# Six split halves of weights instead of four, with raw weights loaded in 1024-column halves

## The chip, the cores and the metric

The kernel runs on one core of one Trainium2 chip. The metric is the device time of one execution in microseconds (us), the median of several runs.

## What is computed

The reference takes 256 tokens of width 1024 through four layers, all in float32. The first block has two layers: a hybrid mixer (sliding-window attention beside a chunked gated delta rule) and a recurrent mixer (a gated linear recurrence), each followed by a layer norm and an MLP with a squared ReLU. The second block has two layers with latent attention, a 31-tap and a 3-tap convolution branch and another such MLP, modulated by vectors that come from large modulation weights; its first layer also carries 256 context tokens.

```python
def sqrelu_mlp(x, w1, w2):
    h = jax.nn.relu(x @ w1)
    return (h * h) @ w2
```

Nearly all the work is x @ w of this kind. The weights are read once each: about 190 MB of layer weights and 50 MB of modulation weights.

## The kernel before

**Products in three passes.** Each float32 operand is split into a rounded high part and the low remainder. A product is then three matmuls: high by high, high by low, low by high. The weights arrive in float32 and are split on the chip.

**Units and halves.** The host packs the weights into units of up to 2048 columns by 128 partitions (1 MB), in the order of their use. Each unit is split in two halves of up to 1024 columns. w_load starts the DMA of a whole unit into one of two raw tiles (tag wr, line 387). w_split takes the next half: ScalarE copies it to the high tile wh (line 407), VectorE subtracts to get the low tile wl (line 408). wh and wl have NW = 4 buffers each. w_next hands out one unit; it first loads one unit further (`while WS.nd < min(u + 2, nus)`) and splits one half further than its own unit (`while WS.nsp < min(first[u + 1] + 1, len(halves))`).

**What frees a buffer.** A raw tile comes free when both of its halves have been split, so the next load waits on VectorE's line 408. A wh or wl buffer comes free when TensorE has done the last matmul that reads it.

**Order of the work.** The program is written as one long list with generators that are woven together by hand. A planner then lays the instructions on the five engine queues: it follows the written order as priority, by its own model of when operands and buffers are ready. high_priority(ahead) moves the splits up that order by ahead places (60 in the mixers of the first block, 0 or as given elsewhere). On the chip each queue runs strictly in the order it was given. All DMAs are issued from one queue, SP: weights, modulation weights (tag wm, line 737, 512 KB each), rows of gains (line 448) and constants.

**Stages.** From about 225 to 425 us, 525 to 690 us and 1460 to 1625 us run the MLPs of 256 tokens, where each weight half is used once; from 950 to 1290 us an MLP over 512 tokens, where each half is used longer. Between them lie the mixers. At each passage into an MLP or mixer the function head (line 534) needs two whole units, that is four halves, at once, and its input comes through a chain on VectorE and ScalarE: layer norm (lines 660 to 670) or post_norm and normed (lines 1389 to 1426), transposes on TensorE (line 366), then to_xT (lines 645 to 649). tm1024 (line 501) is the last product before such a passage; its last two units are read until its very end.

Of the kernel before, what the change touches and what calls it, by code (L numbers as in the profile page):

```python
# [10 lines left out]
F32 = mybir.dt.float32  # L11
# [4 lines left out]
P = 128  # L16
BIG = 1.0e30
SM = 1.0 / math.sqrt(96.0)
NW = 4
LEAD = 96  # L20
TRAIL = 24
ALPHA = 4.0 ** 0.25
# [271 lines left out]
def hybrid_then_mla(ctx: ExitStack, tc: tile.TileContext, a, out, usizes):  # L294
    nc = tc.nc
    V, S, G, T = nc.vector, nc.scalar, nc.gpsimd, nc.tensor
    cpool = ctx.enter_context(tc.tile_pool(name="cpool", bufs=1))
    wpool = ctx.enter_context(tc.tile_pool(name="wpool", bufs=1))
# [39 lines left out]
    def f(ap):  # L338
        return ap.bitcast(F32)
# [32 lines left out]
    nus = len(usizes)  # L372
    halves = []
# [3 lines left out]
    first = [min(n for n, h in enumerate(halves) if h[0] == u) for u in range(nus)] + [len(halves)]  # L377

    def w_load():
        i = WS.nd  # L380
        WS.nd += 1
        r = wpool.tile([P, 2048], F32, tag="wr", bufs=2, name=f"wr{i}")
        n = usizes[i][0]
        parts = 2 if i < 2 else 1
        for j in range(parts):
            o = n // parts * j
            nc.sync.dma_start(out=r[:, o : o + n // parts], in_=a["wp"][i, :, o : o + n // parts])
            if i == 0:
                x_load(j)
        WS.raw[i] = r  # L390

    def x_load(q):
        nc.sync.dma_start(out=xT0[:, 2 * q : 2 * q + 2], in_=a["xT"][:, 2 * q : 2 * q + 2])

    def w_split():
        i = WS.nsp
        WS.nsp += 1
        u, o, n = halves[i]
        while WS.nd <= u:
            w_load()  # L400
        r = WS.raw[u][:, o : o + n]
        h = wpool.tile([P, 1024], F32R, tag="wh", bufs=NW, name=f"wh{i}")
        l = wpool.tile([P, 1024], F32R, tag="wl", bufs=NW, name=f"wl{i}")
        if u in WS.vec:
            V.tensor_copy(h[:, :n], r)
        else:
            S.copy(h[:, :n], r)  # L407
        V.tensor_tensor(l[:, :n], r, f(h[:, :n]), op=SUB)  # L408
        WS.hl[i] = (h[:, :n], l[:, :n])

    class Weights:

# [11 lines left out]
    def w_next(nk, ahead=None):  # L424

        ahead = WS.ahead if ahead is None else ahead
        u = WS.ng
        WS.ng += 1
        assert usizes[u][1] == nk
        while WS.nd < min(u + 2, nus):  # L430
            w_load()
        with tc.high_priority(ahead):
            while WS.nsp < min(first[u + 1] + 1, len(halves)):
                w_split()
        return Weights(nk, [WS.hl.pop(i) for i in range(first[u], first[u + 1])])

    w_load()
    x_load(2)
    x_load(3)
# [37 lines left out]
    def fm_unit(xTs, emit):  # L477

        w = w_next(8)
        for si, xT in enumerate(xTs):  # L480
            ps = psA()
            for m in range(2):
                for k in range(8):
                    fm_acc(ps[:, 256 * m : 256 * m + 256], xT, k, w, k, slice(128 * m, 128 * m + 128), k == 0, k == 7)
            emit(si, ps)

    def tm_group(xTs_tiles, n, nunits, emit):

        pss = [psA() for _ in xTs_tiles]
        per = 8 // nunits  # L490
        for u in range(nunits):
            w = w_next(per)
            for i, (xT, t) in enumerate(xTs_tiles):
                for kk in range(per):
                    k = u * per + kk
                    tm_acc(pss[i][:, :n], xT, k, slice(128 * t, 128 * t + 128), w, kk, slice(0, n), k == 0, k == 7)
                if u == nunits - 1:
                    emit(i, pss[i])
            yield

    def tm1024(xT, done, late, order=(0, 1, 2, 3)):

        pss = [[psA(), psA()] for _ in range(2)]

        def go(n, w, t, cs=(0, 1)):
            for c in cs:
                for kk in range(2):
                    tm_acc(pss[t][c], xT, 2 * order[n] + kk, slice(128 * t, 128 * t + 128), w, kk, slice(512 * c, 512 * c + 512),
                           n == 0 and kk == 0, n == 3 and kk == 1)

        for n in range(2):
            w = w_next(2)
            for t in range(2):
                go(n, w, t)
        w2, w3 = w_next(2), w_next(2)
        for t in range(2):
            for c in ((0,), (1,)):
                go(2, w2, t, c)
                go(3, w3, t, c)
            if t:  # L520
                late.ready(0)
            done(t, pss[t])
# [202 lines left out]
    class WM:  # L725
        tiles, n = {}, 0
# [72 lines left out]
    def run(g):  # L799
        for _ in g:  # L800
            pass

    def hybrid():
# [22 lines left out]
            S.copy(kv[t], ps[:, :264])  # L826

        run(tm_group([(xT, 0), (xT, 1)], 264, 2, kv_emit))
        while WS.nd < 4:
            w_load()  # L830
        nc.sync.dma_start(out=cols, in_=a["cols"])
        nc.sync.dma_start(out=small, in_=a["rows"][ROWS.index("small") : ROWS.index("small") + 1, 0:16].to_broadcast([P, 16]))
        nc.sync.dma_start(out=kcs[1][:, : a["kch"].shape[1]], in_=a["kch"])
# [1088 lines left out]
    def mlp512(Ts, xs, late):  # L1922
# [97 lines left out]
        return T1, ready  # L2020

    xT = hybrid()
    xT = mlp_block1(0, xT, False, rec_consts)
    xT = recurrent(xT)
# [42 lines left out]
```

## Time and profile before

| what | value |
|---|---|
| time, median of 3 runs | 1632.86 us (1632.76 to 1634.14) |
| time of the profiled execution | 1635.88 us |
| span of the profiled execution | 1633.8 us |
| mean granted TensorE clock | 0.991 |
| TensorE busy (matmul) | 1578.0 us, 97% |
| VectorE, ScalarE busy | 1029.0 us, 743.3 us |
| DMA moved | 259.77 MB, mean 159 GB/s |

The time of an execution lies about 2 us above its span, which runs from the first to the last instruction. The clock is the share that TensorE was granted of its full speed. A busy TensorE is not one at its peak, since the ends of matmuls are modelled.

### The profile page before, as it was taken

The numbers are of one execution on the slowest core, as the hardware profiler recorded it, in microseconds if no ns is written. First come the engines' busy times: TensorE is split into PE (matmuls) and PEld (weight loads), VectorE is DVE, ScalarE is ACT, GpSimd is POOL, SyncE is SP. The second block draws the span as 40 slices with busy tenths as digits, with TensorE's granted clock in tenths as the row PEclk, the third lists the DMA queues.
The fourth block names the chain that finished last, engine by engine and source line by source line (L and its number), as shares of the span: only waits on it lengthen the run. The fifth ranks groups of instructions, "written<-read, shape, count | busy, mean of one in ns | idle before, by whom it ended". The sixth has DMA issues, their size and how long they took to land.

```text
span 1633.8 us, 24905 instructions
## 1 busy us (share of the span) xinstructions
PE 1578.0 (97%) x10182; PEld 1358.9 (83%) x10182; DVE 1029.0 (63%) x1593; ACT 743.3 (45%) x1264; POOL 94.8 (6%) x121
## 2 busy tenths in 40 slices
PE   7999999999999999999999999999999999989998
PEld 7866679888878998877877789999999788779997
DVE  6874575556787556768974753444444789775555
ACT  5642244443574445436454543222222475554443
POOL 0021000000000000003010100000000030000000
PEclk9999999999999999999999999999999999989999
DMA  7865475555665554562310432222232262235553
GB/s 289 288 217 172 167 258 196 204 207 191 248 258 181 194 192 169 181 227 80 130 52 27 138 134 89 93 103 85 97 104 79 100 216 107 73 126 201 181 186 124
DMA packets 46946, 259.77 MB, mean 159 GB/s; under 512 B 5600, under 2 KB 5856, under 8 KB 24304
## 3 DMA queue, kind: packets, MB, share of 16 engines
q1 hardware_dynamic: 46832, 258.18, 44.9%
q8 instruction: 80, 1.31, 0.3%
q14 instruction: 34, 0.28, 0.1%
HBM read 257.08 MB, written 1.08 MB: 158 GB/s over the span
## 4 chain that ended last, share of the span: by engine, by line
PE 78%; DVE 8%; ACT 4%; DMA 2%; POOL 1%; issue 1%; POOLq 0%; DVEq 0%; ACTq 0%; SPq 0%
PE pa L342 44%; PE pb L342 27%; PE pm L342 4%; PE pb L366 2%; DVE wl L408 1%; DMA wr<-in_wp_dram 1%; PE pc L366 1%; ACT s L1389 1%; ACT wh L407 1%; DVE s L1583 1%; POOL ti L1395 1%; ACT s L1652 0%; DVE s L645 0%; DVE b L711 0%; DVE xt L1426 0%
## 5 line engine op out<-in xcount | busy, mean ns | idle before, releaser
L408 DVE TENSOR_TENSOR wl<-wr,wh 128x1024 fp32r<-128x1024 f32 (+2 forms) x366 | 443.4, 1217 | 301.4 <-ACT wh L407 288.4
L407 ACT CAST wh<-wr 128x1024 fp32r<-128x1024 f32 (+2 forms) x364 | 376.1, 1041 | 405.8 <-PE pa L342 202.6
L342 PE MATMUL pa<-wh,b 128*128 128x512 f32 (+3 forms) x1456 | 411.1, 365 | 12.5 <-ACT b L816 5.7
L342 PE MATMUL pb<-b,wh 128*128 128x256 f32 x2240 | 406.2, 284 | 0.0
L342 PEld LDWEIGHTS pb<-b,wh 128*128 128x128 f32 x2240 | 352.7, 192 | 7.2 <-issue 3.4
L342 PE MATMUL pb<-b,wl 128*128 128x256 f32 x1120 | 317.8, 284 | 0.0
L342 PEld LDWEIGHTS pa<-wh,b 128*128 128x128 f32 x1456 | 267.6, 195 | 57.1 <-ACT b L648 6.1
L342 PE MATMUL pa<-wl,b 128*128 128x512 f32 (+3 forms) x728 | 258.7, 364 | 8.9 <-DVE wl L408 8.9
L342 PE MATMUL pa<-wh,s 128*128 128x512 f32 x768 | 244.5, 391 | 0.0
L342 PEld LDWEIGHTS pb<-b,wl 128*128 128x128 f32 x1120 | 215.1, 192 | 1.7 <-issue 1.7
L342 PE MATMUL pa<-b,wh 128*128 128x256 f32 x1056 | 199.2, 289 | 3.7 <-ACT wh L407 1.9
L342 PEld LDWEIGHTS pa<-b,wh 128*128 128x128 f32 x1056 | 166.2, 193 | 16.0 <-issue 4.4
L342 PEld LDWEIGHTS pa<-wl,b 128*128 128x128 f32 x728 | 142.3, 195 | 35.3 <-DVE wl L408 13.5
L342 PEld LDWEIGHTS pa<-wh,s 128*128 128x128 f32 x768 | 144.4, 188 | 28.9
L342 PE MATMUL pa<-b,wl 128*128 128x256 f32 x528 | 150.1, 288 | 1.3 <-DVE wl L408 1.3
L342 PE MATMUL pa<-wl,s 128*128 128x512 f32 x384 | 150.4, 392 | 0.0
L342 PEld LDWEIGHTS pa<-b,wl 128*128 128x128 f32 x528 | 101.6, 193 | 8.2 <-DVE wl L408 3.3
L560 DVE TENSOR_TENSOR s<-s 128x512 f32<-128x512 f32 x80 | 54.9, 687 | 50.2 <-ACT s L558 50.2
L342 PE MATMUL pm<-wm,cs_t 128*32 128x512 f32 x384 | 83.2, 606 | 1.9 <-DMA wm<-in_wm_dram 1.7
L342 PEld LDWEIGHTS pa<-wl,s 128*128 128x128 f32 x384 | 72.3, 188 | 14.5 <-DVE wl L408 1.2
L1583 DVE SCALAR_TENSOR_TENSOR s<-cu,cols_sb,s 128x512 f32<-128x512 f32 (+1 forms) x120 | 70.7, 621 | 0.5
L366 PE MATMUL pb<-kc_sb,s 128*128 128x128 f32 x366 | 56.8, 279 | 10.8 <-DVE s L1408 2.5
(278 smaller groups left out, 1391.6 us busy)
## 6 DMA issues: line engine op xcount, KB each, us to landing
wr<-in_wp_dram SPq DMA_DIRECT2D x176, 1024.0 KB, 4.8
wm<-in_wm_dram SPq DMA_DIRECT2D x96, 512.0 KB, 5.2
row<-in_rows_dram SPq DMA_DIRECT2D x10, 512.0 KB, 5.5
wr<-in_wp_dram SPq DMA_DIRECT2D x4, 832.0 KB
s<-in_bg_dram SPq DMA_DIRECT2D x24, 128.0 KB, 5.6
row<-mdr SPq DMA_DIRECT2D x6, 512.0 KB, 3.5
wr<-in_wp_dram SPq DMA_DIRECT2D x4, 264.0 KB, 3.6
b<-in_xT_dram SPq DMA_DIRECT2D x4, 256.0 KB, 6.1
```

Source lines behind the costliest of these rows:

```text
L342: T.matmul(o, l, r, start=start, stop=stop)
L366: T.transpose(o, i, ident)
L407: S.copy(h[:, :n], r)
L408: V.tensor_tensor(l[:, :n], r, f(h[:, :n]), op=SUB)
L560: V.tensor_tensor(q, r, r, op=MUL)
L1389: S.activation(j, x, AF.Square, scale=scale, accum_out=o)
L1395: G.tensor_tensor(r, e, half[:, :1], op=POW)
L1583: V.scalar_tensor_tensor(ac, src, w(k), ac, op0=MUL, op1=ADD)
```

## The change

The raw weights come in halves. A half is one DMA of up to 1024 columns (512 KB) into one of NR = 3 raw tiles of 1024 columns, in place of two tiles of 2048. wh and wl get six buffers each in place of four. w_next splits NW - 3 = 3 halves further than its own unit in place of one. The next load is no longer written at w_next but right behind each split, inside the same high_priority block. At the start three halves are loaded before the first split, and the extra loads ahead of the constants are gone. Per partition the weights' tiles take 60 KB in place of 48.

```diff
-NW = 4
+NW = 6
+NR = 3
...
     def w_load():
+
         i = WS.nd
         WS.nd += 1
-        r = wpool.tile([P, 2048], F32, tag="wr", bufs=2, name=f"wr{i}")
-        n = usizes[i][0]
-        parts = 2 if i < 2 else 1
-        for j in range(parts):
-            o = n // parts * j
-            nc.sync.dma_start(out=r[:, o : o + n // parts], in_=a["wp"][i, :, o : o + n // parts])
-            if i == 0:
-                x_load(j)
+        u, o, n = halves[i]
+        r = wpool.tile([P, 1024], F32, tag="wr", bufs=NR, name=f"wr{i}")
+        nc.sync.dma_start(out=r[:, :n], in_=a["wp"][u, :, o : o + n])
+        if u == 0:
+            x_load(i)
         WS.raw[i] = r
...
     def w_split():
         u, o, n = halves[i]
-        while WS.nd <= u:
-            w_load()
-        r = WS.raw[u][:, o : o + n]
+        r = WS.raw.pop(i)[:, :n]
...
         WS.hl[i] = (h[:, :n], l[:, :n])
+        if WS.nd < len(halves):
+            w_load()
...
     def w_next(nk, ahead=None):
-        while WS.nd < min(u + 2, nus):
-            w_load()
         with tc.high_priority(ahead):
-            while WS.nsp < min(first[u + 1] + 1, len(halves)):
+            while WS.nsp < min(first[u + 1] + NW - 3, len(halves)):
                 w_split()
...
+    w_load()
     w_load()
     x_load(2)
     x_load(3)
...
         run(tm_group([(xT, 0), (xT, 1)], 264, 2, kv_emit))
-        while WS.nd < 4:
-            w_load()
         nc.sync.dma_start(out=cols, in_=a["cols"])
```

## Rows read from the trace of the kernel before

**Rows 1.** The page's engines: busy us, share of the span, instructions.

```profile
PE 1578.0 (97%) x10182; PEld 1358.9 (83%) x10182; DVE 1029.0 (63%) x1593; ACT 743.3 (45%) x1264; POOL 94.8 (6%) x121
```

**Rows 2.** Busy time by stage; then granted clock, DMA share, GB/s.

```profile
0.00:25.00 25.00, 16.47 (x95) 15.52 (x96) 13.21 (x36) 11.66 (x19) 3.27 (x10) 0.93 0.84 294
...
225.00:425.00 200.00, 200.00 (x1261) 173.90 (x1260) 115.79 (x125) 88.83 (x105) 1.84 (x2) 1.00 0.60 211
425.00:525.00 100.00, 92.69 (x632) 80.33 (x631) 84.28 (x126) 60.91 (x95) 1.98 (x2) 0.97 0.58 212
```

**Rows 3.** TensorE's waits over the span: total us, times, longest.

```profile
PE pa L342 <- DVE wl L408: 10.2, 8, 2.4
...
PE pa L342 <- ACT wh L407: 1.9, 1, 1.9
```

**Rows 4.** TensorE's timeline: matmuls before which it idled for weights, and two transposes behind.

```profile
16.83 0.51 PE L342 MATMUL pa<-b,wh 128*128 128x256 f32 x2 [1.89 <-ACT wh L407]
18.09 0.39 PE L342 MATMUL pa<-b,wl 128*128 128x256 f32 x1 [0.75 <-DVE wl L408]
...
437.68 0.39 PE L342 MATMUL pa<-b,wl 128*128 128x256 f32 x1 [0.56 <-DVE wl L408]
...
478.22 0.50 PE L342 MATMUL pa<-wl,b 128*128 128x512 f32 x1 [1.28 <-DVE wl L408]
...
481.72 0.50 PE L342 MATMUL pa<-wl,b 128*128 128x512 f32 x1 [1.85 <-DVE wl L408]
...
508.74 0.39 PE L342 MATMUL pa<-wl,b 128*128 128x256 f32 x1 [2.38 <-DVE wl L408]
...
513.05 0.76 PE L366 MATMUL pb<-kc_sb,xt 128*128 128x128 f32 x4
...
930.09 0.58 PE L342 MATMUL pa<-wl,b 128*128 128x256 f32 x1 [2.22 <-DVE wl L408]
...
933.24 0.60 PE L366 MATMUL pb<-kc_sb,s 128*128 128x128 f32 x4
...
1321.13 0.46 PE L342 MATMUL pa<-wl,b 128*128 128x416 f32 x1 [0.93 <-DVE wl L408]
```

**Rows 5.** Busy time in short stretches behind the waits, columns as in the stages.

```profile
480.00:490.00 10.00, 8.28 (x29) 6.69 (x30) 8.42 (x11) 2.48 (x4) 0.00 (x0) 0.83 0.86 327
510.00:515.00 5.00, 4.76 (x28) 4.53 (x27) 4.27 (x6) 1.07 (x2) 0.99 (x1) 0.66 0.93 315
930.00:935.00 5.00, 4.91 (x30) 4.91 (x31) 4.38 (x10) 1.22 (x3) 1.40 (x1) 0.68 0.73 223
```

**Rows 6.** VectorE's timeline: the ends of the chains that feed the passages.

```profile
488.53 0.69 DVE L1321 TENSOR_TENSOR b<-s,b 128x512 fp32r<-128x512 f32 x1 [0.69 <-ACT b L1320]
...
511.19 1.42 DVE L670 SCALAR_TENSOR_TENSOR xt<-xt,ti,row 128x512 f32<-128x512 f32 x2
...
931.68 0.88 DVE L1408 TENSOR_SCALAR s<-xc,ti 128x512 f32<-128x512 f32 x2 [0.44 <-POOL ti L1395]
```

**Rows 7.** The raw weights at the start: SP's issues, then ScalarE's timeline.

```profile
8.34 4.13 SPq L387 DMA_DIRECT2D wr<-in_wp_dram  x2
...
15.74 1.99 ACT L407 CAST wh<-wr 128x1024 fp32r<-128x1024 f32 x2 [1.60 <-DMA wr<-in_wp_dram]
```

**Rows 8.** Tiles wr and wm: splits (ns min/median/max), then times to landing, wr before wm.

```profile
L408 DVE TENSOR_TENSOR wl<-wr,wh x366: 701/1225/2301, 5.1 to 1617.7; 128x1024 fp32r<-128x1024 f32 x177, 128x832 fp32r<-128x832 f32 x4, 128x528 fp32r<-128x528 f32 x2
L407 ACT CAST wh<-wr x364: 627/1050/1087, 4.4 to 1616.6; 128x1024 fp32r<-128x1024 f32 x176, 128x832 fp32r<-128x832 f32 x4, 128x528 fp32r<-128x528 f32 x2
...
DMA to landing us min/median/max: 3.6/4.8/8.2
...
DMA to landing us min/median/max: 3.4/5.2/8.4
```

**Rows 9.** SP's waits over the span.

```profile
SPq L387 <- DVE wl L408: 1012.2, 163, 18.9
```

**Rows 10.** The chain that ended last, at the passage into the last MLP.

```profile
1434.36 2.27 DVE wl L408 x2
```

## The prediction

> **What bounds the kernel now.** I read the page's engine shares first. TensorE is busy for 1578.0 of 1633.8 us [rows 1], so at most 1633.8 - 1578.0 = 55.8 us of idle time can be won, plus whatever time it ran at a lowered clock. The table by stage comes next. From 225 to 425 us, an MLP, TensorE is busy all the time at full clock, with VectorE at 115.79 of 200 us and DMA at a share of 0.60 [rows 2]: earlier weights are worth nothing there, nor in the other MLPs, where the same pattern repeats. What the change can give lies in the passages between the MLPs. TensorE's own waits tell how much of the idle time is put down to weights: 10.2 us in 8 waits for the low half and 1.9 us in one wait for the high half, 12.1 us in all [rows 3]. The timeline says where: two at the start, three from 437 to 482 us, and one each at 508, 930 and 1321 us [rows 4]. The 43.7 us of other idle time (norm chains, attention) are not the change's business unless the splits get in their way.
>
> The waits have a second price. After three of them the granted clock falls from its level of 2.4 GHz to that of 1.2 GHz for a while: the mean is 0.83 over 480 to 490 us, 0.66 over 510 to 515 and 0.68 over 930 to 935 [rows 5]. A stretch of length T with mean clock c has lost T x (1 - c): 1.7, 1.7 and 1.6 us, 5.0 us together. The ceiling of the direct gain is 12.1 + 5.0 = 17.1 us, 1.0% of the time.
>
> **The change part by part.** *Two more split buffers and a lookahead of three halves.* With four buffers, w_next can have the unit in hand and one half of the next. With six it has the next unit whole and a half of the one after. A split still waits for the same event: under either rule the last half asked for at w_next reuses the buffer of the first half of the unit just consumed. So the work per release is the same, one ScalarE copy of 1.05 us and one VectorE subtraction of 1.23 us [rows 8], and what comes out of it is needed two halves later. The 366 splits remain 366; no busy time is added. At each passage the unit's first two halves are ready before the last product of the stage before has ended, where now all four of a head's halves are split at its very end. Now each wait in turn, with what is late next when it goes:
>
> - 437 to 490 us. The three waits take 0.56 + 1.28 + 1.85 = 3.69 us [rows 4], and the clock 1.7 us [rows 5], together 5.4. VectorE is busy 84.28 of 100 us in this stretch [rows 2], but its slack before 425 us takes the two extra splits. What can be late next is the last quarter of the mixer's output, ready at 488.53 + 0.69 = 489.2 us [rows 6]. TensorE reaches it after 50 more matmuls of 512 columns behind the wait at 481.72; a column a cycle at 2.4 GHz is 0.21 us each, and with the clock loss that is 481.7 + 10.7 + 1.7 = 494.1 us. So 4.9 us can be moved before that bites. I take 4.9; the bounds are 0 (the splits come no earlier on a saturated VectorE) and 5.4.
> - 508 us. 2.38 us of waiting and 1.7 us of clock, but what TensorE does next, the transposes of the second token tile, needs line 670, which ends at 511.19 + 1.42 = 512.6 us [rows 6]; they start at 513.05 now [rows 4]. I take 0.4; bounds 0 and 4.1.
> - 930 us. In the same way line 1408 ends at 931.68 + 0.88 = 932.6 [rows 6] and TensorE's transposes start at 933.24 [rows 4]. I take 0.7; bounds 0 and 2.22 + 1.6 = 3.8.
> - 1321 us. 0.93 us, with a norm chain close behind. I take 0.5; bounds 0 and 0.93.
>
> *Raw weights in halves.* At the start the second unit pair is issued at 8.34 us, when the first raw tile comes free, and its split begins only at 15.74, ended by the DMA [rows 7]: 7.4 us for a whole megabyte behind the other first loads. Its first half alone is half the bytes: at the 294 GB/s of that stage [rows 2] the second 0.52 MB are 1.8 us. The two waits there are 1.89 + 0.75 = 2.64 us [rows 4]. The fourth half (the second unit's other part) now waits for the first split, behind the load of a["cols"], 130 KB, which costs 0.5 us at that rate. I take 1.5 of the 2.64, because the mixer's VectorE chains follow; bounds -0.5 and 2.64.
>
> The loads become 366, one for each split, in place of about half as many. SP waits 1012.2 us for line 408 alone [rows 9], and that hides their issue; it would cost only if a modulation load stood behind it with TensorE waiting. What stands behind a blocked load on SP are the modulation weights, rows of gains and constants; the block is now for half a unit's split at a time, in place of a whole unit's, so I cost it at nothing, with 0 to 2 us as bounds.
>
> Whether a ring of three halves feeds the splits: three halves must go round in the time in which TensorE eats three. The MLP stage issues 1261 matmuls in 200 us [rows 2], and a pair of units takes 48 + 24 = 72 of them, 11.4 us, so three of its four halves last 8.6 us. One turn is landing + copy + subtraction. A 512 KB transfer lands in 3.4 us at least and 5.2 in the median among other traffic, a whole unit in 4.8 in the median [rows 8]. 3.4 + 1.05 + 1.23 = 5.7 us, with the median 7.5: under 8.6. The old ring's turn, 4.8 + 1.05 + 2 x 1.23 = 8.3 of 11.4 us for four halves, is no looser. Cost nothing while a landing stays under 8.6 - 2.3 = 6.3 us.
>
> The trace shows half-size transfers costing no bandwidth: 480 to 490 us, where 512 KB modulation loads are under way, moves 327 GB/s at a DMA share of 0.86 [rows 5], 380 at full share, and the MLP stage with whole units 211 at 0.60 [rows 2], 352. The Trainium skill speaks against the change here: its page "DMA: Bandwidth & Descriptors", section "Rules for kernel authors", asks for at least 1 MiB per DMA for the highest bandwidth. By that rule the loads would take more of the DMA engines, and the start would be the place to pay. By the rows it is nothing.
>
> **The sum.** 4.9 + 0.4 + 0.7 + 0.5 + 1.5 = 8.0 us. Against the profiled execution's 1635.88 us that gives 1627.9. That execution lies 3.0 us above the median of the runs, 1632.86, and the gain is taken from the median: 1624.9 us.
>
> **The rivals.**
>
> *The wait only changes its name (no change).* On VectorE the splits at 478 and 508 us are late because it works without a pause, and the norm chains end within 0.4 and 0.7 us of the waits that would go. If the splits ahead fall into the same saturated stretch, only the start is left: 1632.86 - 1.5 = 1631.4 us. For it: 84.28 of 100 us [rows 2]. Against it: at 478 the chain ends 4.9 us before it is needed.
>
> *The splits ahead push in front of the norm chains (slower).* They are now written two halves earlier, before the norm of the stage that ends, so the planner ranks them above it. The chain at 1434.36 shows what that looks like: two subtractions, 2.27 us, in front of the step that TensorE waits for [rows 10]. If two more halves come there, each passage loses 2 x 1.23 = 2.45 us of VectorE. There are seven passages: 7 x 2.45 - 8.0 = 9.2 us, 1642 us. It decides from five passages on, since 5 x 2.45 = 12.3 is more than the gain and the limit of measurement, 8.0 + 3.3. Against it: a split still happens only when a buffer is freed, and the number freed at a passage is the same.
>
> *The ring of three halves, or the smaller transfers, become the bound (slower).* From a landing of 6.3 us on, each further 0.5 us costs 0.5 us per three halves. The three MLPs of 256 tokens have 192 halves, 64 turns: 32 us less the gain, 1657 us. If instead a half-size transfer took as long as its uncontended landing alone, 2 x 3.4 against 4.8 us or 1.42 times the DMA time, the MLPs' share of 0.60 would be 0.85, still hidden, and only the first 25 us at 0.84 [rows 2] would run over, by 0.19 x 25 = 4.8 us. Against it: the landings and rates above. The page's rule on 1 MiB, named above, would act through this rival.
>
> **How the numbers follow.** The forecast of a gain has 0.63, with a range of its own from 1616 (the ceiling of 17.1 us) to 1629.5. The renamed wait has 0.17, of which 0.01 is large enough to be a gain, the splits before the norm chains 0.14, the ring 0.06. A difference of 0.2%, 3.3 us, is about what a measurement here can tell from none. Faster than that: 0.63 + 0.01 = 0.64. Within it: 0.16. Slower: 0.14 + 0.06 = 0.20. The range that leaves out no more than 2 in 10 reaches from 1616 through the case of no change to 1640, just short of the full price of the second rival and without the third.
>
> **What the profile after would show.** Right: TensorE's waits for lines 407 and 408 fall from 12.1 us to 4 or less, the clock stays at its full level from 480 to 490 us, the first unit's splits begin near 13 us in place of 15.74, the MLP stages keep their length, and raw loads of 512 KB land in about 3.5 us. The waits at 508 and 930 turn into ones for the transposes' inputs, with the same instants after them. Wrong: waits for line 408 that stay in number at the same places (first rival); a longer time from the last matmul of a stage to the first of the next, with line 408 in the chain before lines 645 to 670 (second); ScalarE waiting on the raw weights' DMA inside the MLPs, and TensorE on line 407 there (third). I would be wrong above all if the planner, given other ready times, lays the queues out anew in stages that have nothing to do with weights.

## The result

The change makes the kernel slower: 1646.81 us (median of 4 runs, 1644.7 to 1650.59) against 1633.06 (4 runs, 1632.76 to 1634.14), a ratio of 1.0086 with a 95% interval of 1.0066 to 1.0105, or 14 us. The forecast was 1624.9 us in a range from 1616 to 1640: the time lies above the range, and the sign is the other one.

### The profile page after: what moved, and what is told of

It reads as the page before. It is cut to its first block, busy times and chain, and to the rows that moved or that the text cites. A ratio compares the mean times of both kernels' runs of the same rounds, so it can differ in the third digit from the quotient of the medians.

```text
span 1645.5 us, 25334 instructions
## 1 busy us (share of the span) xinstructions
PE 1592.7 (97%) x10182; PEld 1363.7 (83%) x10182; DVE 1032.0 (63%) x1593; ACT 745.0 (45%) x1264; POOL 95.6 (6%) x121
## 4 chain that ended last, share of the span: by engine, by line
PE 81%; DVE 7%; ACT 3%; POOL 1%; issue 1%; DMA 1%; POOLq 0%; DVEq 0%; ACTq 0%; SPq 0%
PE pa L343 45%; PE pb L343 27%; PE pm L343 5%; PE pb L367 3%; DVE wl L405 1%; PE pc L367 1%; ACT s L1385 1%; POOL ti L1391 1%; DMA wr<-in_wp_dram 1%; DVE s L1579 1%; ACT wh L404 1%; DVE s L643 0%; DVE s L1404 0%; DVE b L709 0%; DVE b L647 0%
## 5 line engine op out<-in xcount | busy, mean ns | idle before, releaser
L404 ACT CAST wh<-wr 128x1024 fp32r<-128x1024 f32 (+2 forms) x364 | 377.2, 1042 | 451.2 <-PE pa L343 200.2
L343 PE MATMUL pa<-wh,b 128*128 128x512 f32 (+3 forms) x1456 | 409.9, 363 | 11.1 <-ACT b L646 5.6
L343 PE MATMUL pm<-wm,cs_t 128*32 128x512 f32 x384 | 96.5, 618 | 4.7 <-DMA wm<-in_wm_dram 4.7
L367 PE MATMUL pb<-kc_sb,s 128*128 128x128 f32 x366 | 59.9, 288 | 13.2 <-POOL s L1482 6.4
```

Source lines behind the costliest of these rows:

```text
L343: T.matmul(o, l, r, start=start, stop=stop)
L367: T.transpose(o, i, ident)
```

## The profile after

The execution profiled after the change took 1647.52 us with a span of 1645.5 us, 11.7 us more than the span before. The page's engines, then TensorE's waits over the span (us in total, times, longest):

```profile
PE 1592.7 (97%) x10182; PEld 1363.7 (83%) x10182; DVE 1032.0 (63%) x1593; ACT 745.0 (45%) x1264; POOL 95.6 (6%) x121
```

```profile
PE pb L367 <- POOL s L1482: 6.4, 2, 4.1
...
PE pm L343 <- DMA wm<-in_wm_dram: 4.7, 1, 4.7
PE pb L343 <- DVE s L852: 3.2, 2, 2.9
...
PE pa L343 <- DVE wl L405: 1.8, 3, 0.8
...
PE pa L343 <- ACT wh L404: 0.2, 1, 0.2
```

The waits that the change was to remove are gone: 12.1 us for split weights before [rows 3], 1.8 + 0.2 = 2.0 now. But TensorE is busy 14.7 us longer than in [rows 1] with the same 10182 matmuls. One group of the page holds nearly all of that (busy us, mean ns, idle before and its releaser), here before and after:

```profile
L342 PE MATMUL pm<-wm,cs_t 128*32 128x512 f32 x384 | 83.2, 606 | 1.9 <-DMA wm<-in_wm_dram 1.7
```

```profile
L343 PE MATMUL pm<-wm,cs_t 128*32 128x512 f32 x384 | 96.5, 618 | 4.7 <-DMA wm<-in_wm_dram 4.7
```

These are the modulation matmuls of mods(), which the edit does not touch: 48 steps of four (r = 0 to 3), each on its own 32 columns of TensorE, two records each in the trace. Their mean duration hardly changes, so the work did not get slower. It is cut up differently. The timeline after the change, 101 to 113 us, then two rows of the timeline before:

```profile
101.61 1.06 PE L343 MATMUL pm<-wm,cs_t 128*32 128x512 f32 x6
...
103.69 1.05 PE L343 MATMUL pm<-wm,cs_t 128*32 128x512 f32 x2
...
107.75 1.06 PE L343 MATMUL pm<-wm,cs_t 128*32 128x512 f32 x8
```

```profile
98.43 1.05 PE L342 MATMUL pm<-wm,cs_t 128*32 128x512 f32 x2
102.50 1.06 PE L342 MATMUL pm<-wm,cs_t 128*32 128x512 f32 x8
```

Three matmuls in a row (x6), one alone (x2) and four (x8) all take 1.05 to 1.06 us: the four column groups work side by side, so one alone holds TensorE as long as four. I call an unbroken row of them a run. Counted from start of run to start of the next other matmul over the whole timeline, an undisturbed run of up to four costs 0.98 us and one of five to eight 0.86 more. The planner lays the 192 matmuls out in 70 runs before and 81 after, where 48 would do:

| | runs | runs of over 4 | the rest | TensorE's time for them |
|---|---|---|---|---|
| before | 70 x 0.98 = 68.6 | 8 x 0.86 = 6.9 | 7.4 | 82.9 us |
| after | 81 x 0.98 = 79.4 | 9 x 0.86 = 7.7 | 12.5 | 99.6 us |

That is 16.8 us more; the page's busy time, which leaves idle time out, has 13.3 more. The rest is idle time inside a run (0.1 us before, 4.7 after), idle time right behind one, which ends when another step's operand comes (3.9 and 3.8), and what single runs took beyond the two figures. The 4.7 us are a single wait. First SP's timeline (time in the second column is that of issuing, blocked or not), then SP's waits from 449 to 451.2 us, then TensorE's timeline:

```profile
437.55 11.13 SPq L386 DMA_DIRECT2D wr<-in_wp_dram  x3
450.82 0.33 SPq L735 DMA_DIRECT2D wm<-in_wm_dram  x1
451.25 0.53 SPq L386 DMA_DIRECT2D wr<-in_wp_dram  x1
451.82 1.53 SPq L735 DMA_DIRECT2D wm<-in_wm_dram  x3
```

```profile
SPq L735 <- PE pm L343: 2.2, 1, 2.2
```

```profile
449.74 1.92 PE L343 MATMUL pm<-wm,cs_t 128*32 128x512 f32 x14
456.37 1.91 PE L343 MATMUL pm<-wm,cs_t 128*32 128x512 f32 x2 [4.71 <-DMA wm<-in_wm_dram]
```

Seven matmuls were ready, the eighth's weights were not. A wm tile holds the weights of two matmuls, there are four such buffers, and the seven matmuls had used all four. The load for the eighth needed a buffer that this very run was still reading: SP waited for the run's first matmuls and issued it at 450.82 us. The raw halves ahead of it did not hold it, the last was issued by 437.55 + 11.13 = 448.68. The planner put eight in a row there all the same, and TensorE stood still for 4.71 us.

So the span's 11.7 us are 14.7 of busy time, 13.3 of them in this group, less 3.0 of idle time (55.8 us before, 52.8 now). In the idle time 12.1 - 2.0 = 10.1 us of weight waits are gone. In their place, the wait for modulation weights is 4.7 us where it was 1.7, those for line 1482 (1486 before) are 6.4 where they were 2.2, and one at 43.12 us is new.

The clock gives nothing back. It is at its full level where the forecast wanted it, but over the whole span its mean is 0.987, where it was 0.991. By the forecast's own T x (1 - c) that is 1645.5 x 0.013 = 21.4 us lost in place of 1633.8 x 0.009 = 14.7: some 7 us more where 5.0 were to come back, though part of it falls on time in which TensorE stood idle. Two of the new places; busy us by engine, granted clock, DMA share and GB/s:

```profile
40.00:45.00 5.00, 2.15 (x12) 1.95 (x11) 3.70 (x7) 4.65 (x12) 0.00 (x0) 0.83 0.70 284
...
750.00:760.00 10.00, 5.61 (x18) 2.20 (x19) 8.31 (x16) 6.85 (x16) 6.46 (x13) 0.66 0.56 178
```

In both stretches TensorE had stood idle, as before the dips in [rows 5]. From 750 to 760 us the clock was 0.83 before. The first stretch is a split's doing. ScalarE's timeline, 39 to 43 us, and TensorE's:

```profile
39.69 1.05 ACT L404 CAST wh<-wr 128x1024 fp32r<-128x1024 f32 x1 [3.19 <-DMA wr<-in_wp_dram]
40.65 0.62 ACT L901 ACTIVATE s<-s 128x512 f32<-128x512 f32 x1
41.18 1.26 ACT L868 ACTIVATE b<-b,gc 128x128 f32<-128x128 f32 x4
```

```profile
43.12 1.97 PE L343 MATMUL pb<-b,s 128*128 128x128 f32 x8 [2.85 <-DVE s L852]
```

A split that was written early sits at the head of ScalarE's queue and waits 3.19 us for a half that has not landed. The mixer's own steps stand behind it, VectorE waits for line 901, and TensorE for VectorE's line 852.

## The experiments

The expectations weigh three theories. Theory 1: the loss is the new layout of the modulation matmuls. Theory 2: it is the raw halves, which come late and hold ScalarE. Theory 3: it is the splits, written further ahead and pushed in front of the norm chains.

The kernel before ran again beside each group (medians of 1633.2 to 1635.1 us), so the ratios are those to quote; their intervals are about 2 to 4 us to either side, and differences of that size are not told apart. "Weight waits" are TensorE's waits for both split lines, "modulation" is its time for these matmuls, counted as above with the idle time in and behind the runs; both are from the profile of the run.

| run | split halves, raw tiles | median us | ratio to before, 95% | runs | modulation us | weight waits us |
|---|---|---|---|---|---|---|
| before | 4, two whole | 1633.06 | | 70 | 82.9 | 12.1 |
| after | 6, three halves | 1646.81 | 1.0086 (1.0066 to 1.0105) | 81 | 99.6 | 2.0 |
| e3 | 4, three halves | 1641.02 | 1.0049 (1.0033 to 1.0065) | 71 | 90.7 | 10.5 |
| e4 | 5, two whole | 1618.94 | 0.9917 (0.9894 to 0.9940) | 70 | 80.5 | 3.8 |
| e8 | 5, three halves | 1640.42 | 1.0034 (1.0019 to 1.0048) | 75 | 91.4 | 3.5 |
| e13 | 5, five halves | 1627.14 | 0.9964 (0.9951 to 0.9978) | 73 | 90.5 | 2.2 |
| e17 | 6, four halves | 1635.88 | 1.0015 (1.0002 to 1.0028) | 76 | 91.0 | 1.7 |
| *precedence -1* | | | | | | |
| e10 | 4, two whole | 1617.40 | 0.9899 (0.9883 to 0.9914) | 56 | 70.3 | 11.0 |
| e9 | 6, three halves | 1621.92 | 0.9917 (0.9900 to 0.9934) | 56 | 78.9 | 3.4 |
| *kept together by a lead* | | | | | | |
| e6 | 4, two whole | 1609.15 | 0.9846 (0.9825 to 0.9867) | 44 | 53.0 | 13.5 |
| e7 | 5, two whole | 1599.23 | 0.9782 (0.9764 to 0.9801) | 42 | 54.4 | 6.2 |
| e11 | 5, three halves | 1614.61 | 0.9880 (0.9867 to 0.9892) | 44 | 59.9 | 7.3 |
| e14 | 5, four halves | 1597.54 | 0.9774 (0.9749 to 0.9799) | 40 | 55.4 | 3.2 |
| e12 | 5, five halves | 1597.14 | 0.9764 (0.9751 to 0.9778) | 40 | 55.3 | 3.2 |
| e5 | 6, three halves | 1604.77 | 0.9819 (0.9800 to 0.9838) | 41 | 58.7 | 2.7 |
| e18 | 6, four halves | 1607.19 | 0.9841 (0.9820 to 0.9863) | 40 | 55.1 | 1.7 |
| *modulation loads on POOL* | | | | | | |
| e15 (bound) | 5, three halves | 1635.23 | 1.0003 (0.9992 to 1.0014) | 42 | 61.5 | 8.4 |
| e16 | 6, three halves | 1663.86 | 1.0181 (1.0163 to 1.0199) | 75 | 101.7 | 3.9 |

**Binding the four in a block (e1, e2).** One block around the four matmuls of a step, in the changed kernel and in the one before:

```diff
-            for r in range(4):
-                with tc.high_priority(-10):
+            with tc.high_priority(-10), tc.tile_critical():
+                for r in range(4):
                     mm(ps[32 * r : 32 * r + 32, :], cs_t[:, k, :], ...)
```

> The changed kernel with the four matmuls of each modulation step (r = 0..3, one 32-column group of the array each) bound into one block that nothing can come between, so 192 of them stand in 39 runs where the changed kernel has 81 and the kernel before 70. Theory 1 (the loss is the new layout of these matmuls: in the changed kernel they hold TensorE for 99.6 us, before for 82.9, and a run of one takes 1.06 us where a run of four takes 1.00): they hold about 48 x 1 = 48 us, the time falls by 40 to 52 us to about 1595 to 1607, and it ends 6 to 12 us below the kernel before with the same edit, since the waits for split weights (13.0 us before, 2.7 after) stay gone. Theory 2 (the loss is the raw halves: ACT's splits wait 79.8 us for them where they waited 25.3, and with each stands what is queued behind it on ACT): the modulation gain comes to both kernels alike, and this one stays 8 to 14 us above the kernel before with the same edit. Theory 3 (splits written two halves further ahead push in front of the norm chains): as theory 2.

> The kernel before with the same binding of the four matmuls of a step: 39 runs for 70. Theory 1: they hold about 48 us for 82.9, so about 1633 - 35 = 1598, or some us more where a block waits for the later of its two wm tiles; it ends 6 to 12 us above the changed kernel with the same edit. Theories 2 and 3: it ends 8 to 14 us below the changed kernel with the same edit.

Both miss by far and alike: 1752.68 and 1753.03 us. The block has a price of its own that hides everything else. TensorE's weight loads in the first of the two:

```profile
PEld pm L343 <- issue: 124.8, 48, 6.1
```

At each of the 48 blocks its queue stops for 2.6 us in the mean, waiting for nothing that the profile shows. These two runs say nothing on the theories.

**One part of the change at a time (e3, e4).** The first is the changed kernel with `NW = 4`; the second the kernel before with

```diff
-NW = 4
+NW = 5
...
-            while WS.nsp < min(first[u + 1] + 1, len(halves)):
+            while WS.nsp < min(first[u + 1] + NW - 3, len(halves)):
```

> The changed kernel with four split halves again (NW = 4, so one half ahead as in the kernel before); of the change only the raw halves through a ring of three are left. Its modulation matmuls stand in 71 runs, one more than before. Theory 1: these cost what they cost before (about 83 us), the weight waits are those of before, and it lies within 5 us of the kernel before, 1629 to 1638. Theory 2: it keeps the loss or adds to it, since the deeper split buffers that could hide late halves are gone: 1645 to 1655. Theory 3: the loss is gone, as under theory 1; the next run parts 1 from 3.

> The kernel before with five split halves and splits written two halves ahead; raw units stay whole, 1 MB, in a ring of two. Its modulation matmuls stand in 70 runs, as before. Theory 1: these cost what they cost before, and part of the weight waits goes: 1623 to 1630. Theory 2: the weight waits go and no half is late: 1621 to 1627. Theory 3: the norm chains are pushed back by one more half each: 1637 to 1645.

Five halves with whole raw units gain 13.6 us (0.83%), somewhat more than theories 1 and 2 gave them, where theory 3 wanted a loss: splits written two halves ahead, in place of one, cost nothing that shows (three ahead come with e5). The raw halves alone lose 8.0 us, more than theory 1 had expected and less than theory 2. Where they go this run does not tell. The modulation time is 90.7 - 82.9 = 7.8 us longer, but 4.9 of that is idle time right behind the runs (8.8 us against 3.9), in which TensorE waits for other steps; the page has the group busy for 85.9 us against 83.2.

**The matmuls bound without a block (e5, e6, e7) and five halves (e8).** The fourth matmul, whose tile arrives last, is issued in the old place, and the other three right behind it:

```diff
-            for r in range(4):
-                with tc.high_priority(-10):
-                    mm(ps[32 * r : 32 * r + 32, :], cs_t[:, k, :], ...)
+            with tc.high_priority(-10):
+                lead = mod_mm(3)
+            with tc.issue_after(lead.ins), tc.high_priority(4000):
+                for r in range(3):
+                    mod_mm(r)
```

> The changed kernel with the modulation matmuls kept together in another way, without the block of e1 (whose 48 blocks each held TensorE's queue for about 2.6 us, a cost of the tool and not of the matmuls): r = 3, whose tile arrives last, is issued first, and the other three right behind it with precedence over all else. 41 runs for 81. Theory 1 (layout of the modulation matmuls): they hold about 47 us for 99.6, so 1595 to 1605, and 6 to 12 us below the kernel before with the same edit. Theory 2 (raw halves: loads late, ACT held): about 1600 as well, but 5 to 10 us above the kernel before with the same edit. If the matmuls' room is not on the path that sets the end, neither moves.

> The kernel before with the same edit: 44 runs for 70, about 47 us of TensorE for 82.9, so 1597 to 1607 under every theory. Theory 1 wants it 6 to 12 us above the changed kernel with the edit, theory 2 some 5 to 10 us below it.

> The kernel before with five split halves written two ahead (1618.9 us by itself) and the modulation matmuls kept together: 42 runs for 70, about 47 us for 80.5. Both theories: the two gains add, 1585 to 1595. If the deeper splits gained through the layout alone, it is no faster than the kernel before with only the matmuls kept together.

> The changed kernel with five split halves (two ahead): against the kernel before with five (1618.9), it differs in the raw halves and their ring of three alone. Theory 1: its modulation matmuls stand in 75 runs, between four halves (71, 1641.0) and six (81, 1646.8): 1630 to 1640 for 90 to 95 us of them. Theory 2: the raw halves cost what they cost at four split halves, 8 us: 1627. Theory 3 (splits too far ahead): one half less ahead regains half of what six lost against four, so 1643.

Now every step is one run, and the page's group shrinks to these lines, in the changed kernel and in the one before:

```profile
L773 PE MATMUL pm<-wm,cs_t 128*32 128x512 f32 x384 | 52.4, 631 | 1.4 <-DMA wm<-in_wm_dram 1.4
```

```profile
L775 PE MATMUL pm<-wm,cs_t 128*32 128x512 f32 x384 | 50.3, 603 | 0.0
```

By the ratios (times 1633) the changed kernel gains 43.6 us from it and the kernel before 25.2. The order of the two is turned round: with the same binding the change is 4.4 us ahead, 1604.77 against 1609.15. Their intervals overlap a little, their executions do not (1604.6 to 1606.9, 1607.54 to 1612.85). Theory 1 had asked for 6 to 12, theory 2 for a loss of 5 to 10. The gains of five halves and of the binding nearly add up, 35.6 us in e7 for 13.6 and 25.2; 1599.23 lies 10.5 us below e6 and 4 above the range expected. Without the binding, five halves with a ring of three stand 19 us above five with whole units (e8, e4). Theory 1's 1630 to 1640 for e8 was met at its edge, theory 2's 1627 was not; but of the 19 us only 91.4 - 80.5 = 10.9 are modulation time.

**One number in the planner's precedence (e9, e10).** `high_priority(-10)` around the modulation matmuls becomes `high_priority(-1)`, in both kernels; nothing else.

> The changed kernel with one number altered: the modulation matmuls stand 1 instead of 10 behind in the planner's precedence. No weight, load or ring is touched; they stand in 56 runs for 81. Theory 1: 25 runs fewer at 0.98 us each are 24 us off 1646.8, so about 1622; and since the kernel before with the same number has 56 runs too, it ends 4 to 10 us below that one. Theory 2: the raw halves' loss of about 8 us stays against the kernel before with the same number.

> The kernel before with the same number altered: 56 runs for 70, so 14 us off 1634: about 1620 under both theories. Theory 1 wants it 4 to 10 us above its counterpart of the changed kernel, theory 2 some 8 us below it.

Both times came as worked out from the runs: 1621.92 for 1622, 1617.40 for 1620. So a number that touches no weight moves the changed kernel by 25 to 28 us (by the medians and by the ratios). But with 56 runs each the change is not ahead: by the ratios it is 2.9 us behind, within their intervals. The stall of 456 us is still there in the changed kernel, at another time:

```profile
436.46 1.92 PE L343 MATMUL pm<-wm,cs_t 128*32 128x512 f32 x14
443.09 1.91 PE L343 MATMUL pm<-wm,cs_t 128*32 128x512 f32 x2 [4.72 <-DMA wm<-in_wm_dram]
```

What its runs take beyond 0.98 and 0.86 us is 13.7 us against 8.5, and this stall is most of the difference. The granted clock is lower too, 0.985 to 0.991 in e9's executions and 0.992 to 0.995 in e10's. Theory 1 in its narrow form (the count of runs) was not enough; the ring of raw halves had to be tried by itself.

**The ring by itself (e11 to e14).** Five split halves. e11, e12 and e14 are bound by the lead, with `NR = 3`, 5 and 4; e13 has the planner's layout and `NR = 5`.

> The changed kernel with five split halves and the modulation matmuls kept together (44 runs). Against the kernel before with five and the same binding (1599.2, 42 runs) it differs in the raw halves and their ring of three alone, with the layout held. Theory 1 alone: within 3 us of 1599. Theory 2: the halves have a price of their own, 5 to 10 us, so 1604 to 1609; the six-half kernel with the binding stands at 1604.8.

> The run before with a ring of five raw halves for three. If the ring of three is too short (a 512 KB landing of 4.4 us, asked for only when a split frees a buffer), this takes back what e11 lost against 1599.2. If halves cost through their number (twice as many transfers of half the size on the one queue that also loads the modulation weights), it stands where e11 stands, or worse. If e11 lost nothing, nothing moves.

> The changed kernel with five split halves and a ring of five raw halves, modulation matmuls as the planner lays them (73 runs). Beside e8 (ring of three, 75 runs, 1640.4) it tells the ring's price in the changed kernel's own layout. Ring as a cause of its own: 1622 to 1628, back to what five whole-unit halves gave (1618.9) or near it. Layout alone: two runs of matmuls fewer, so 1636 to 1640.

> Modulation matmuls kept together, five split halves, a ring of four raw halves, which is the memory of the two whole units before. Ring three: 1614.6, ring five: 1597.1. If a half is late because its load waits for a buffer, most of the gain comes with the fourth: 1597 to 1602. If the difference is scatter of the planner's order, it can lie anywhere from 1597 to 1615 and says nothing of size; 40 runs of matmuls stand in it as in the ring of five.

With three raw halves 1614.61 us, with four 1597.54, with five 1597.14, with two whole units 1599.23. So with the matmuls bound loading in halves is free, and three buffers in place of four cost 17 us, more than either theory gave e11. In the planner's layout a ring of five takes back 11.4 us (e8, e13), with nearly the same modulation time (91.4 and 90.5), so the ring's price does not come through these matmuls. The other 7.7 us between e13 and five halves from whole units (e4) do go with modulation time, 90.5 - 80.5 = 10.0. ScalarE's waits for raw weights follow the ring; e11, then e14, e12, then five whole-unit halves (e7):

```profile
ACT wh L404 <- DMA wr<-in_wp_dram: 80.9, 56, 4.2
```

```profile
ACT wh L404 <- DMA wr<-in_wp_dram: 13.6, 15, 2.2
```

```profile
ACT wh L404 <- DMA wr<-in_wp_dram: 5.7, 5, 2.4
```

```profile
ACT wh L407 <- DMA wr<-in_wp_dram: 77.3, 61, 5.7
```

The last of them warns against reading this row as a price: e7 waits as long as e11 and is 15 us faster. What counts is what TensorE then waits for. In e11 and in e14, the rows that differ most:

```profile
PE pm L773 <- DMA wm<-in_wm_dram: 5.5, 2, 4.0
PE pa L343 <- DVE wl L405: 5.0, 6, 1.7
PE pb L367 <- DVE b L979: 4.6, 2, 3.0
PE pb L367 <- DVE xt L668: 2.4, 3, 1.2
PE pa L343 <- ACT wh L404: 2.3, 2, 1.3
```

```profile
PE pa L343 <- DVE wl L405: 3.2, 5, 1.2
...
PE pb L367 <- DVE b L979: 1.4, 2, 0.9
...
PE pm L773 <- DMA wm<-in_wm_dram: 0.6, 2, 0.4
PE pb L367 <- DVE xt L668: 0.3, 1, 0.3
```

Late modulation weights 4.9 us, late splits 4.1, the steps of line 979 and 668 3.2 and 2.1. All of TensorE's waits add up to 57.9 us in e11 and 46.8 in e14, 11.1 of the 14.8 us by which the spans differ. The ring's price is paid in many small waits between the MLPs. ScalarE's waits for raw halves differ there too: from 25 to 225 us, ahead of the first MLP, they are 31.7 us in e11 and 4.2 in e14.

**The modulation loads in another queue (e15, e16).** `nc.sync.dma_start(out=wm, ...)` becomes `nc.gpsimd.dma_start(out=wm, ...)`, in e11 and in the changed kernel.

> e11 (five split halves, ring of three, 1614.6) with the 96 modulation loads issued from the POOL queue, so that none stands behind a half's load that waits for its buffer. If the ring acts through these loads: 1598 to 1603. If it acts through late halves (splits on ACT and what is queued behind them): within 3 us of 1614.6.

> The changed kernel itself with only the modulation loads taken to the POOL queue (75 runs of matmuls for 81). If the stall of 5 us at 456 and the late loads are the cause, they go, and with them the 6 runs: 1630 to 1636. If the cause is late halves, only the 6 runs go: about 1641.

Both are slower than what they were made from, which none of the expected outcomes allowed: 1635.23 us for 1614.61, 1663.86 for 1646.81. From POOL's queue the loads take longer to land, 5.8 us in the median for 5.5 (e15, e11) and 5.9 for 4.7 (e16, after), and TensorE's wait for them in e15 is now

```profile
PE pm L773 <- DMA wm<-in_wm_dram: 10.9, 6, 3.6
```

where e11 had 5.5. POOL's queue also stood for 332.8 us waiting for free wm buffers in e15, with POOL's own steps behind, so the two runs change more than the place of the loads:

```profile
POOL wm L735 <- PE pm L773: 332.8, 36, 80.3
```

One thing they settle. The stall of 456 us is there in e16 as well, with no raw half in the loads' queue; TensorE's timeline, then POOL's:

```profile
460.10 1.92 PE L343 MATMUL pm<-wm,cs_t 128*32 128x512 f32 x14
467.78 1.91 PE L343 MATMUL pm<-wm,cs_t 128*32 128x512 f32 x2 [5.76 <-DMA wm<-in_wm_dram]
```

```profile
461.56 1.76 POOL L735 DMA_DIRECT2D wm<-in_wm_dram  x3 [34.24 <-PE pm L343]
```

The load again waits for the run's own first matmuls, so this stall is one of the layout and of the four wm buffers, and not of SP's queue. Whether SP's queue carries the rest of the ring's price the runs don't tell; they tell that POOL's is no cure.

**A fourth raw half at six split halves (e17, e18).** `NR = 4` in the changed kernel and in e5, its memory taken from the half-row temporaries (tag s2, nine buffers to seven).

> The changed kernel with a ring of four raw halves, paid for with two of nine temporaries of 2 KB; its modulation matmuls stand in 76 runs for 81. If the ring's price is that of five split halves, 13 to 17 us: 1629 to 1634, within noise of the kernel before or just under it. If six split halves already cover the ring: 1641 to 1647, the five runs at most. Fewer temporaries can only work against it.

> The same with the modulation matmuls kept together (40 runs; ring of three 1604.8). Ring's price as at five split halves: 1588 to 1592, the fastest of all. If six split halves cover the ring: 1602 to 1605. If the two temporaries were needed: above 1605.

In the changed kernel the fourth buffer takes back 11.6 us, of which 99.6 - 91.0 = 8.6 are modulation matmuls; it stands level with the kernel before to within 0.3%, between the two outcomes expected. With the matmuls bound it takes back nothing, which was expected if the two temporaries were needed. Weight waits are down to 1.7 us there, but TensorE now waits 2.8 us for line 1010 of POOL, a row that is not in e5, and 6.0 for ScalarE's line 1653 where e5 had 4.0. Whether the two temporaries do this was not tried.

The fastest versions are e12 and e14, 1597.14 and 1597.54 us, 37 to 39 us below the kernel before: five split halves, raw halves in a ring of four or five, and the modulation matmuls kept together. Five halves from whole units (e7) stand within 2 us of them.

## Why the prediction was wrong

- *The direct gain: right.* The weight waits fell to 2.0 us, under the 4 that were named as the sign. Five halves alone already gain 13.6 us (e4), more than the 8.0 of the sum. With the matmuls bound each further half gave 10 us (e6 to e7, e11 to e5). Two terms were too small. Counted over TensorE's matmuls outside modulation, the changed execution's lag falls from 8.8 to 4.5 us around 508 us (term 0.4, upper bound 4.1; modulation matmuls laid there had just raised it from 5.4) and from 8.0 to 4.7 around 930 us (0.7 and 3.8). The norm chains did not come earlier: line 668 (670 before) ends at 520.2 us for 512.6, line 1404 (1408 before) at 940.6 for 932.6. But TensorE does not need them as soon: the planner put the transposes behind more weight matmuls, at 519.65 us for 513.05 and 940.25 for 933.24. The sum had taken TensorE's order there as given. The clock's part of the gain did not come: its dips at 480, 510 and 930 us are gone, but others came, and the mean fell from 0.991 to 0.987.

- *The start: right in direction.* The split that began at 15.74 [rows 7] begins at 12.12, and the waits of 1.89 and 0.75 us [rows 4] are down to one of 0.76. At 25 us the changed execution is 3.1 us ahead, where 1.5 was taken, with 2.64 as upper bound.

- *The modulation matmuls: the step that failed.* "I cost it at nothing, with 0 to 2 us as bounds" priced only their loads and not their places. They cost 16.8 us more in the profiled execution, 13.3 of it busy time. Binding them takes 43.6 us from the changed kernel and 25.2 from the one before, and turns a loss of 14.0 us into a gain of 4.4, whose sign the overlapping intervals leave open. Of this difference of 18.4 us, 11.0 are their time (40.9 us saved against 29.9). The profiled spans themselves differ by 12.5 us (40.7 saved against 28.2), so this is most of what the profiles show; the rest lies between these executions and their medians. The forecast named this case in its last words on what would make it wrong ("lays the queues out anew") and gave it no price and no chance. The price could have been read: the group of 83.2 us was on the page before, and a single matmul beside a row of four in its timeline (98.43 and 102.50 us above) would have shown that 48 steps need only some 48 us, so that a new layout could give or take tens of them.

- *The ring of three: the second step that failed.* "Cost nothing while a landing stays under 8.6 - 2.3 = 6.3 us" was worked out for the steady MLP, and there it held: in the three MLPs behind 525 us the two executions keep their distance to 0.4 us. Between the MLPs it did not. With five halves the ring of three costs 16 to 19 us in the bound layout, by the ratios (e11 against e7, e14 and e12), and 11.4 in the planner's (e8 against e13). The sum compared one turn of the ring with TensorE's pace in the MLP. It left out that at the passages four halves are wanted at once; the old ring held four, the new one three. That this is how the price arises is my reading, which no run shows by itself. At six halves, those of the change, the ring's price apart from the layout is not shown either (e17, e18). The forecast's rival of this kind had the right part and the wrong place, with 0.06.

- *Splits ahead of the norm chains: refuted.* e4 splits two halves ahead in place of one and gains, and three ahead beat two with the matmuls bound (e5, e11). A split at the head of ScalarE's queue does harm where its half hasn't landed (39.69 us); whether the ring or the split's place in the queue is to blame there was not tried apart. The renamed wait came only in small part: 0.77 us for line 668 at 511.56 and 0.44 for line 1404 at 929.35, where 2.38 and 2.22 us of weight waits went.

- *Half-size transfers: right that they cost nothing.* A half lands in 4.4 us in the median (3.5 was forecast, a unit takes 4.8 [rows 8]). With the matmuls bound, whole units against a ring of four halves, 1599.23 and 1597.54, shows no loss by size. The section "Rules for kernel authors" of the page "DMA: Bandwidth & Descriptors" of the Trainium skill, which asks for at least 1 MiB per DMA for the highest bandwidth, speaks for whole units; these two times show no gain from them.

Step by step, from the ratios: in the bound layout the fifth half gives -10.5 us (e6, e7), raw halves in a ring of three +16.0 (e11), the sixth half -10.0 (e5), together -4.4. In the planner's layout the same steps are -13.6 (e4), +19.1 (e8) and +8.5 (the change), together +14.0. Each step is uncertain by some 3 to 5 us. It is the sixth half that changes sign there, and 99.6 - 91.4 = 8.2 us of modulation matmuls come with it.

What stays open: why the ring of three delays just these steps in the mixers, whether SP's one queue carries the delay, what the ring costs at six halves where it is not paid for with temporaries, and how much of the loss goes through the lower clock, which no run holds fixed.

## What to carry to other kernels

When a planner lays out the queues, an edit's first cost is the new layout of work that it doesn't touch; look for groups whose time depends on their neighbours (here four matmuls that share one pass) and bind them before you judge the edit. A row of them longer than their ring of operands stalls (4.71 us here). Size a ring by the burst it has to feed and by what the old one held, not by the steady pace of the longest stage. To see which part of a change pays, cross the parts under a held layout: here two gains of 10 us and a loss of 16 lay behind one small number.

## What the runs showed of the hardware

- Four 128x512 float32 matmuls on four 32-column groups of TensorE take 1.06 us, as does one of them alone. A kernel that scatters them pays for it: 99.6 us for 192 of them after the change, 58.7 when the same kernel keeps them together (e5).
- A block that the planner may not interleave (e1) stops TensorE's queue for 2.6 us each time, 124.8 us in 48 blocks.
- The same 512 KB modulation loads issued from POOL's queue left TensorE waiting 10.9 us for them, from SP's 5.5 (e15, e11); landing took 5.8 us in the median for 5.5.
